# Softmax reciprocals applied to attention outputs by way of DRAM, with two steps of the feed-forward's side work moved

## The chip, the cores and the metric

The kernel runs on one core of a Trainium2 chip. The metric is the time of one execution in microseconds (us) on the device. Before the change three runs took 1823.91 to 1831.17 us, with a median of 1830.18.

The core has TensorE (PE; its weight loads are shown apart as PEld), VectorE (DVE), ScalarE (ACT), GpSimd (POOL) and SyncE (SP), which here only issues DMAs. The engines run side by side; each takes its own instructions in order and waits on semaphores.

## The reference

One encoder layer is applied with the same parameters to a prompt of 1024 tokens and a sample of 512, each token a row of 1024 float32. With a depth of 1 the layer is neighbourhood attention (16 heads of 64) followed by SwiGLU:

```
h = rms_norm(x, norm_mix)
x = x + neighbourhood_attention(h, w_qkv, rpb) @ w_o
x = x + swiglu(rms_norm(x, norm_ffn))        # (silu(a @ w_gate) * (a @ w_up)) @ w_down
y = rms_norm(x, norm_final)
```

Tokens lie on a grid 64 wide. A query sees a window of up to 8 rows by 16 columns of keys, with a bias per head and offset. For each head and query

```
s = q . k * scale + bias          (-inf outside the window)
p = softmax(s);   o = p @ v
```

## The kernel before, in words

**Precision.** Every matrix product is done in three passes on float32 operands split in two parts: a rounded high part (ACT casts) and the difference to the raw value (DVE subtracts, reading the raw and the high part). `split` (L139 to L145) does this, so most operands cost one ACT and one DVE instruction; L141 and L142 are those lines.

**V and the biases** come first (0 to 157 us): all V rows are computed and stored in DRAM (`v_d`), and the relative biases are laid out in DRAM as tables.

**Attention** (157 to 727 us) works on pairs of heads: eight pairs, each with two query groups of the prompt, then the eight pairs again with the one group of the sample. A group has two steps, so there are 32 prompt steps and 16 sample steps. A step handles two column blocks j of two heads each, that is four score tiles of 128 queries by 384 keys (256 in the sample). In `scores` (L391) the four tiles are computed on TensorE (`pss`, L397). For each tile DVE adds the bias, negates and takes the row minimum (L405), ACT takes the exponential with a row sum (L408), DVE takes the reciprocal of the row sum (L410), and the tile is multiplied by it, on DVE for the first head (L412) and on ACT for the second (L414). `flip` (L418) transposes the result on TensorE by 128x128 blocks (`ptt`, L423); ACT casts the high part out of PSUM (L426) and DVE takes the difference (L427). The score tiles and the transposed tiles come from the same pool of four PSUM banks (tag S), so the next step's scores wait until L427 has read the banks of this one.

In `step` (L477) the products with V of the *previous* step (`weighted`, L431, `po`) follow the scores of the present one, and `collect` (L438) puts the three parts of each head together: ACT copies one part into `tmp` (L444), DVE adds a second (L445) and the third (L447), the latter straight into `oT`, with 64 partitions for each head of the pair. Every second step POOL stores `oT` to `o_d` in DRAM (L462). `tmp` has two buffers.

Between these parts stand fillers on TensorE: the projections of the next pair's queries and keys (`pg`, L335), and in the sample stage the output projection of the prompt tokens (`pgo`, L593). They keep TensorE busy while the softmax is on its way.

`Chores` load raw weights and V rows ahead on SP's queue: four DMAs for a V job (L381), one for a weight block (L150). There are two raw buffers, so the next load starts when a split has freed one. Two bias tiles are loaded ahead on the same queue (L208 to L218), with a fill by POOL (L207, L211).

**The feed-forward** takes the tokens in two chunks of 768, each as two halves of 384, with the matrix products arranged after Winograd's form of Strassen's scheme: seven half-size products instead of eight, with sums and differences of operands (`operands`, L650) and of results. Each chunk has 11 units; a unit has 14 products (L822, 12 matmuls each), seven for the gate and seven for the up weights. Its results are multiplied (L885), summed on POOL (L889 to L892) and stored by seven DMAs that POOL issues (L894).

Side work runs between the products as generators. `ticks` (L911) gives such a generator one turn after every second product. In the first chunk's units these turns prepare the second chunk (`pair1`, L739): three pairs of token tiles; for each tile `norm2` (L672) loads the rows (L674, on ACT's queue), takes the squares (L677), the mean (L679, DVE), the root (L681, POOL) and the scaling (L683, ACT), and transposes (L690, L691); then the operands go to DRAM. In the last unit of the first chunk and around it they are reloaded as the second chunk's operands (`reload`, L899). In the second chunk's units the turns form the differences of the down weights (`down_sums`, L752): for each of 11 pairs of row blocks two loads, two DVE subtractions (L766, L768), two POOL subtractions (L771, L773) and two stores to `wt_d`, in five turns. From 1490 us on the down projection reads the stored products and weights back (L1066).

**What sets the order.** Each engine's instruction order is fixed when the program is built: the framework orders the traced instructions by its own estimate of when each can run, and the place in the program only decides between those that are ready. So work can run ahead of its place. In the first chunk, the loads of a pair's two tiles are five turns apart in the code, and the trace has them 1.43 us apart (950.34 and 951.77 us).

Of the kernel before, what the change touches and what calls it, by code (L numbers as in the profile page):

```python
# [18 lines left out]
P = 128  # L19
# [36 lines left out]
def body(tc, xp, xs, g_mix, g_ffn, g_fin, w_qkv, rpb, w_o, w_g, w_u, w_d, yp, ys):  # L56
# [9 lines left out]
    with es:  # L66
# [10 lines left out]
        o_d = dr.tile([HP, P, T], F32, name="o_d")  # L77
        x1_d = dr.tile([T, D], F32, name="x1_d")
# [312 lines left out]
        def scores(q, k, krow, nrow, j, bias):  # L391
            n = nrow * 32
            pss = [psum("S", "pss") for _ in range(2)]
            for i, (a, b) in enumerate(PASS):
                for h, pt in enumerate(pss):
                    kv = k[h * HD:(h + 1) * HD, b].rearrange("p (r c) -> p r c", c=GW)
                    nc.tensor.matmul(pt[:, :n], q[h * HD:(h + 1) * HD, a, j].rearrange("p r i -> p (r i)"),  # L397
                                     kv[:, krow:krow + nrow, BS[j]:BS[j] + 32],
                                     start=(i == 0), stop=(i == 2))
            yield  # L400
            out = []
            for h, pt in enumerate(pss):
                s = ap.tile([P, 384], F32, tag="s", name="s", bufs=4)
                mx = stat.tile([P, 1], F32, tag="mx", name="mx")
                nc.vector.tensor_tensor_reduce(s[:, :n], pt[:, :n], bias(h), -1.0, 3.0e38,  # L405
                                               ALU.add, ALU.min, accum_out=mx)
                sm = stat.tile([P, 1], F32, tag="sm", name="sm")
                nc.scalar.activation(s[:, :n], s[:, :n], AF.Exp, bias=mx, scale=-1.0, accum_out=sm)  # L408
                ri = stat.tile([P, 1], F32, tag="ri", name="ri")
                nc.vector.reciprocal(ri, sm)  # L410
                if h == 0:
                    nc.vector.tensor_scalar(s[:, :n], s[:, :n], ri, None, ALU.mult)  # L412
                else:
                    nc.scalar.mul(s[:, :n], s[:, :n], ri)  # L414
                out.append(s)
            yield out
# [21 lines left out]
        def collect(pos, dst):  # L438
            for h in range(2):
                m, o = (0, HD) if h == 0 else (HD, 0)  # L440
                pv = pos[h].rearrange("p (g z q) -> p g z q", g=2, z=2)
                tmp = ap.tile([P, 2, P], F32, tag="tmp", name="tmp")
# [3 lines left out]
                tv = t.rearrange("p g (r i) -> p g r i", i=16)  # L446
                nc.vector.tensor_tensor(dst(h), tv, pv[m:m + HD, :, 1].rearrange("p g (r i) -> p g r i", i=16),  # L447
                                        ALU.add)

        def steps(hp, g, q, k, v, n, store):  # L450
# [4 lines left out]
            for jj in range(2):  # L455
                sc = []
                for j in (jj * 2, jj * 2 + 1):
                    if j != 2:
                        b = next_bias()
                    sc.append(lambda b=b, j=j: scores(q, k, 4 * (g == 1), 4 * n, j, lambda h: b[:, h, :n * P]))  # L460
                yield dict(s=sc, n=n, jj=jj, v=v, dst=lambda h, jj=jj: ov[h * HD:(h + 1) * HD, jj * 2:jj * 2 + 2],
# [15 lines left out]
        def step(st, fill):  # L477

            sc = [x() for x in st["s"]] if st else []
            for x in sc:  # L480
                next(x)
            ss = [next(x) for x in sc]
            fill(0)
            if prev:
                p, pT = prev.pop()
# [3 lines left out]
                collect(pos, p["dst"])  # L489
# [6 lines left out]
            if st:  # L496
                prev.append((st, pT))
# [174 lines left out]
        def norm2(t, xn, xt):  # L672

            nc.scalar.dma_start(out=xn, in_=x1_d[t * P:(t + 1) * P, :])  # L674
            yield
            ms = stat.tile([P, 1], F32, tag="ms", name="ms")
            nc.scalar.activation(xt.rearrange("p k t -> p (k t)"), xn, AF.Square, accum_out=ms)  # L677
            me = stat.tile([P, 1], F32, tag="me", name="me")
            nc.vector.tensor_scalar(me, ms, 1.0 / D, EPS, ALU.mult, ALU.add)  # L679
            rs = stat.tile([P, 1], F32, tag="rs", name="rs")  # L680
            nc.gpsimd.tensor_tensor(rs, me, mhalf, ALU.pow)  # L681
            yield
            nc.scalar.mul(xn, xn, rs)  # L683
            yield
            for b in range(2):
                ks = slice(b * 4, b * 4 + 4)
                pt = psum("S", "pt")
                for kk in range(4):
                    k = b * 4 + kk
                    nc.tensor.transpose(pt[:, kk * P:(kk + 1) * P], xn[:, k * P:(k + 1) * P], ident)  # L690
                nc.vector.tensor_tensor(xt[:, ks], pt.rearrange("p (k t) -> p k t", k=4),  # L691
                                        gT[:, ks].rearrange("p (k o) -> p k o", o=1).to_broadcast([P, 4, P]),
                                        ALU.mult)
                yield

# [4 lines left out]
        def pair0(j):  # L700
            xs = []
            for t in (j, 3 + j):
                xn = np_.tile([P, D], F32, tag="xn", name="xn", bufs=3)
                xt = np_.tile([P, KB, P], F32, tag="xt", name="xt")
                for _ in norm2(t, xn, xt):
# [33 lines left out]
        def pair1(j):  # L739
            xs = []  # L740
            for n, t in enumerate((CT + j, CT + 3 + j)):
                xn = temp(2 * n)
                xt = temp(2 * n + 1).rearrange("p (k t) -> p k t", k=KB)
                yield from norm2(t, xn, xt)
                xs.append(xt)
# [188 lines left out]
        for p in range(NP):  # L934
            unit(1, p, hops2, tick if p else idle, None if 0 < p < NP - 1 else lambda n: None)
# [194 lines left out]
```

## Time and profile before

| | |
|---|---|
| median of three runs | 1830.18 us |
| the profiled execution | 1828.39 us |
| its span, first to last instruction | 1826.6 us |
| mean granted TensorE clock | 0.987 |
| attention, prompt | 157 to 484 us |
| attention, sample | 484 to 727 us |
| rest of the output projection, first chunk prepared | 727 to 797 us |
| gate and up products, both chunks | 797 to 1490 us |
| down projection and final norm | 1490 to 1819 us |

Times in rows of the profile are counted from the start of the span. A row of a group gives line, engine, operation, output and inputs with their shapes and the count, then the busy time in us and the mean of one in ns, then the engine's idle time just before these instructions and who ended it. A row of the timeline gives the start and the length in us; a bracket at its end gives the idle time before it and its releaser. A row of waits gives the total in us, how often, and the longest. The busy time of PE counts matmuls that overlap in the pipeline, so it does not show a slower pace. A releaser is inferred from semaphore events.

### The profile page before, as it was taken

Reading aid. Unit: us, or ns where it says so; the run is one execution under the profiler, and the core shown is the slowest. Engines: PE = TensorE matmul, PEld = TensorE weight load, DVE = VectorE, ACT = ScalarE, POOL = GpSimd, SP = SyncE. Lnnn points to the kernel's source line nnn. Section 1 sums busy time; section 2 is a strip of 40 time slices with the busy share of each in tenths; the row PEclk is TensorE's granted clock in tenths of the full one; section 3 lists DMA queues with packets and bytes.
Section 4 is the critical chain, followed back from the end, with each engine's and each line's share of the span. In section 5 each row is a group of like instructions: output and inputs, shape, how many; then the busy total and the mean of one; then the engine's idle time right before and its main releaser. Section 6 shows DMA issues by size and latency. Waiting matters only on the chain.

```text
span 1826.6 us, 25898 instructions
## 1 busy us (share of the span) xinstructions
PE 1755.7 (96%) x9178; PEld 1534.0 (84%) x9178; DVE 1222.2 (67%) x2263; ACT 869.9 (48%) x1742; POOL 441.4 (24%) x513
## 2 busy tenths in 40 slices
PE   7999999999999999999998999899999999999998
PEld 6887777777767878889998999899999988888886
DVE  4401887777887666667777877999777756546643
ACT  4411776767785554543443435433444435433423
POOL 1121000000130000103323343575424252005300
PEclk9999999999999999999999999899999999999999
DMA  7754333333465443643552635788343259645633
GB/s 242 220 187 157 108 108 101 104 117 108 125 203 155 139 145 121 196 162 120 173 167 93 209 107 168 257 295 287 112 136 122 78 191 322 194 153 165 215 103 107
DMA packets 229858, 295.60 MB, mean 162 GB/s; under 512 B 27648, under 2 KB 173824, under 8 KB 229728
## 3 DMA queue, kind: packets, MB, share of 16 engines
q1 hardware_dynamic: 205744, 215.94, 39.0%
q0 software_dynamic: 21248, 69.62, 10.4%
q10 hardware_dynamic: 2736, 8.39, 1.4%
q8 instruction: 72, 1.18, 0.3%
q14 instruction: 58, 0.48, 0.1%
HBM read 218.45 MB, written 87.97 MB: 168 GB/s over the span
## 4 chain that ended last, share of the span: by engine, by line
PE 69%; DVE 10%; DMA 9%; ACT 4%; issue 4%; POOL 2%; SPq 2%; DVEq 0%; ACTq 0%; POOLq 0%
PE pd L1066 17%; PE pa L822 15%; PE pg L335 8%; PE pd L822 7%; PE pgv L281 6%; PE pgo L593 5%; DMA vr<-v_d 4%; PE pb L822 4%; PE pss L397 3%; PE po L434 2%; PE ptt L423 2%; SPq L381 2%; DMA t<-ffn_w_down 1%; DMA wr<-na_w_qkv 1%; ACT s L408 1%
## 5 line engine op out<-in xcount | busy, mean ns | idle before, releaser
L1066 PE MATMUL pd<-wd,go 128*128 128x512 f32 x1386 | 324.7, 396 | 4.1 <-DVE wd L142 3.4
L1066 PEld LDWEIGHTS pd<-wd,go 128*128 128x128 f32 x1386 | 260.6, 188 | 68.0 <-DVE wd L142 4.8
L822 PE MATMUL pa<-h,ws 128*128 128x384 f32 x1056 | 202.9, 340 | 13.1 <-ACT c L847 10.7
L335 PE MATMUL pg<-hTp,whl 128*128 128x512 f32 x768 | 203.5, 409 | 0.0
L822 PEld LDWEIGHTS pa<-h,ws 128*128 128x128 f32 x1056 | 187.0, 191 | 16.4 <-ACT c L847 12.7
L822 PE MATMUL pd<-h,ws 128*128 128x384 f32 x1056 | 198.9, 336 | 0.1
L822 PEld LDWEIGHTS pd<-h,ws 128*128 128x128 f32 x1056 | 185.9, 189 | 0.5 <-ACT c L851 0.5
L142 DVE TENSOR_TENSOR ws<-wt,ws 128x1024 fp32r<-128x1024 f32 x88 | 114.7, 1304 | 96.7 <-ACT ws L141 96.5
L335 PEld LDWEIGHTS pg<-hTp,whl 128*128 128x128 f32 x768 | 140.4, 192 | 34.5 <-issue 7.7
L822 PE MATMUL pa<-h,wa 128*128 128x384 f32 x792 | 151.5, 344 | 9.3 <-DVE c L854 9.2
L822 PEld LDWEIGHTS pa<-h,wa 128*128 128x128 f32 x792 | 141.9, 192 | 12.3 <-DVE c L854 11.7
L593 PE MATMUL pgo<-wo,oh 128*128 128x512 f32 x576 | 138.9, 392 | 1.3 <-DVE oh L142 1.3
L141 ACT CAST go<-gr 128x768 fp32r<-128x768 f32 x84 | 65.6, 782 | 150.7 <-PE pd L1066 112.4
L408 ACT ACTIVATE s<-s,mx 128x384 f32<-128x384 f32 (+1 forms) x192 | 109.1, 570 | 54.3 <-DVE mx L405 54.1
L142 DVE TENSOR_TENSOR wa<-wr,wa 128x512 fp32r<-128x512 f32 x132 | 123.6, 948 | 11.5 <-ACT wa L141 10.4
L142 DVE TENSOR_TENSOR go<-gr,go 128x768 fp32r<-128x768 f32 x84 | 81.5, 971 | 71.6 <-ACT go L141 70.2
L894 POOL DMA_DIRECT2D gop_d<-c x66 | 50.6, 766 | 320.8 <-DVE c L885 315.9
L593 PEld LDWEIGHTS pgo<-wo,oh 128*128 128x128 f32 x576 | 107.4, 188 | 24.3 <-DVE oh L142 1.8
L141 ACT CAST wa<-wr 128x512 fp32r<-128x512 f32 x132 | 81.8, 621 | 92.4 <-PE pb L822 45.2
L141 ACT CAST ws<-wt 128x1024 fp32r<-128x1024 f32 x88 | 92.5, 1052 | 68.6 <-issue 47.0
L335 PE MATMUL pg<-hTs,whl 128*128 128x512 f32 x384 | 105.7, 411 | 1.6 <-DVE q L346 1.6
L822 PE MATMUL pb<-h,wa 128*128 128x384 f32 x528 | 101.3, 340 | 4.3 <-ACT wa L141 4.1
(159 smaller groups left out, 2954.4 us busy)
## 6 DMA issues: line engine op xcount, KB each, us to landing
wr<-ffn_w_gate SPq DMA_DIRECT2D x44, 512.0 KB
wr<-ffn_w_up SPq DMA_DIRECT2D x44, 512.0 KB
wr<-na_w_qkv SPq DMA_DIRECT2D x38, 512.0 KB
gop_d<-gs POOLq DMA_DIRECT2D x88, 192.0 KB, 5.8
gr<-gop_d SPq DMA_DIRECT2D x42, 384.0 KB
gr<-gop_d SPq DMA_DIRECT2D x42, 320.0 KB
gop_d<-c POOLq DMA_DIRECT2D x66, 192.0 KB, 2.5
vr<-v_d SPq DMA_DIRECT2D x192, 64.0 KB
```

The source lines that it names most:

```text
L141: nc.scalar.copy(hi, raw)
L142: nc.vector.tensor_tensor(lo, raw, f32(hi), ALU.subtract)
L281: nc.tensor.matmul(pg, hh[a][:, k, c:c + P], wv[k // 2][b][:, k % 2], start=(k == 0 and i == 0), stop=(k == KB - 1 and i == 2))
L335: nc.tensor.matmul(pg, w[:, a, k, :], h[b][:, k, c:c + 512], start=(k == 0 and i == 0), stop=(k == KB - 1 and i == 2))
L381: nc.sync.dma_start(out=raw[:, j * P:(j + 1) * P], in_=src[:, BS[j]:BS[j] + 32, :])
L397: nc.tensor.matmul(pt[:, :n], q[h * HD:(h + 1) * HD, a, j].rearrange("p r i -> p (r i)"), kv[:, krow:krow + nrow, BS[j]:BS[j] + 32], start ...
L408: nc.scalar.activation(s[:, :n], s[:, :n], AF.Exp, bias=mx, scale=-1.0, accum_out=sm)
L423: nc.tensor.transpose(pt[:, c * P:(c + 1) * P], s[:, c * P:(c + 1) * P], ident)
L593: nc.tensor.matmul(pg, ohs[k // 4][:, a, k % 4], wo[:, b, k, n * 512:(n + 1) * 512], start=(k == 0 and i == 0), stop=(k == KB - 1 and i == 2))
L822: nc.tensor.matmul(bank[:, :HT], a(y, k), b[:, z, k], start=start and k == 0 and i == 0, stop=k == KB // 2 - 1 and i == 2, skip_group_chec ...
L894: nc.gpsimd.dma_start(out=gop_d[i, 3 * c:3 * c + 3, :, p].rearrange("j q t -> q j t"), in_=a.rearrange("q (j t) -> q j t", j=3))
L1066: nc.tensor.matmul(pd, go[:, y, i - a], wds[m, i][:, z], start=(i == 0 and k == 0), stop=(i == NP - 1 and k == 2))
```

## The change

Three edits:

1. *Attention.* `scores` leaves the exponentials unnormalised and writes the four row sums of a step into one tile of 128x4. After the scores `reciprocals` takes all four reciprocals at once, stores them on SP's queue into a DRAM array `ri_d`, turned so that the queries lie along a row, and loads them back on the same queue into `rt`, one load for each head, with the row repeated on the head's 64 partitions. One step later `collect` adds the three parts in `tmp`, and POOL multiplies `tmp` by `rt` into `oT`. `tmp` has one buffer and holds both heads.
2. *Second chunk's preparation.* `norm2` takes a list of tiles. For a pair it loads both, then takes square, mean and root of each, leaves a turn empty, scales both, and then transposes both. A pair has 14 turns, as before.
3. *Down weights' differences.* The turns for `down_sums` begin with the third unit of the second chunk, not with the second.

```
 def scores(q, k, krow, nrow, j, bias, sm):
...
-                nc.scalar.activation(s[:, :n], s[:, :n], AF.Exp, bias=mx, scale=-1.0, accum_out=sm)
-                ri = stat.tile([P, 1], F32, tag="ri", name="ri")
-                nc.vector.reciprocal(ri, sm)
-                if h == 0:
-                    nc.vector.tensor_scalar(s[:, :n], s[:, :n], ri, None, ALU.mult)
-                else:
-                    nc.scalar.mul(s[:, :n], s[:, :n], ri)
+                nc.scalar.activation(s[:, :n], s[:, :n], AF.Exp, bias=mx, scale=-1.0, accum_out=sm[:, h:h + 1])
...
+        def reciprocals(sm, slot):
+            ri = stat.tile([P, 4], F32, tag="ri", name="ri")
+            nc.vector.reciprocal(ri, sm)
+            nc.sync.dma_start(out=ri_d[slot].rearrange("u h q -> q (u h)"), in_=ri)
+            rt = ap.tile([P, 2, P], F32, tag="rt", name="rt")
+            for h in range(2):
+                nc.sync.dma_start(out=rt[h * HD:(h + 1) * HD],
+                                  in_=ri_d[slot, :, h].rearrange("(o u) q -> o u q", o=1).to_broadcast([HD, 2, P]))
+            return rt
...
-        def collect(pos, dst):
+        def collect(pos, dst, rt):
+            tmp = ap.tile([P, 2, P], F32, tag="tmp", name="tmp", bufs=1)
             for h in range(2):
...
-                tmp = ap.tile([P, 2, P], F32, tag="tmp", name="tmp")
                 t = tmp[m:m + HD]
                 nc.scalar.copy(t, pv[o:o + HD, :, 0])
                 nc.vector.tensor_tensor(t, t, pv[m:m + HD, :, 0], ALU.add)
-                tv = t.rearrange("p g (r i) -> p g r i", i=16)
-                nc.vector.tensor_tensor(dst(h), tv, pv[m:m + HD, :, 1].rearrange("p g (r i) -> p g r i", i=16),
-                                        ALU.add)
+                nc.vector.tensor_tensor(t, t, pv[m:m + HD, :, 1], ALU.add)
+            nc.gpsimd.tensor_tensor(dst, tmp.rearrange("p g (r i) -> p g r i", i=16),
+                                    rt.rearrange("p g (r i) -> p g r i", i=16), ALU.mult)
...
-        def norm2(t, xn, xt):
+        def norm2(tiles):
+            rs = []
+            for t, xn, xt in tiles:
+                nc.scalar.dma_start(out=xn, in_=x1_d[t * P:(t + 1) * P, :])
+            yield
+            for t, xn, xt in tiles:
+                ms = stat.tile([P, 1], F32, tag="ms", name="ms")
+                nc.scalar.activation(xt.rearrange("p k t -> p (k t)"), xn, AF.Square, accum_out=ms)
+                me = stat.tile([P, 1], F32, tag="me", name="me")
+                nc.vector.tensor_scalar(me, ms, 1.0 / D, EPS, ALU.mult, ALU.add)
+                rs.append(stat.tile([P, 1], F32, tag="rs", name="rs"))
+                nc.gpsimd.tensor_tensor(rs[-1], me, mhalf, ALU.pow)
+                yield
+            yield
+            for (t, xn, xt), r in zip(tiles, rs):
+                nc.scalar.mul(xn, xn, r)
+                yield
+            for t, xn, xt in tiles:
+                for b in range(2):
...
         for p in range(NP):
-            unit(1, p, hops2, tick if p else idle, None if 0 < p < NP - 1 else lambda n: None)
+            unit(1, p, hops2, tick if p > 1 else idle, None if 0 < p < NP - 1 else lambda n: None)
```

54 lines of the change are left out of this document (21 added, 33 removed).

## Prediction

> **What bounds the kernel now.** I read the busy times of the page first, then the table by stages, then in each stage with idle time the waits of TensorE, and last the timeline around the longest of them.
>
> ```profile
> PE 1755.7 (96%) x9178; PEld 1534.0 (84%) x9178; DVE 1222.2 (67%) x2263; ACT 869.9 (48%) x1742; POOL 441.4 (24%) x513
> ```
> ```profile
> 157.00:484.00 327.00, 318.24 (x1799) 253.74 (x1797) 246.41 (x700) 219.74 (x534) 26.16 (x59) 0.99 0.38 114
> 484.00:727.00 243.00, 231.39 (x1257) 185.25 (x1257) 174.45 (x509) 147.58 (x386) 31.26 (x32) 0.99 0.48 147
> 860.00:1010.00 150.00, 141.53 (x794) 139.91 (x793) 109.84 (x150) 62.71 (x101) 54.00 (x58) 0.95 0.44 140
> 1110.00:1300.00 190.00, 175.90 (x968) 171.67 (x968) 171.11 (x192) 77.29 (x127) 109.18 (x91) 0.97 0.73 246
> 1300.00:1440.00 140.00, 140.00 (x805) 139.64 (x804) 102.64 (x134) 57.09 (x96) 51.13 (x54) 1.00 0.37 113
> ```
>
> TensorE is busy for 96% of the span, so only its stalls can be won. The second block is the table by stages (window, its length, then PE, PEld, DVE, ACT, POOL busy, granted clock, DMA share, GB/s): prompt attention, sample attention, the stage in which the second chunk is prepared, the change of chunks, and a quiet stretch for comparison. PE is idle for 8.8, 11.6, 8.5, 14.1 and 0.0 us in them. That is 43 us, and the three edits touch just these four stages. "Busy" hides more: after a stall the matmuls run slower for a while.
>
> ```profile
> 274.76 3.05 PE L335 MATMUL pg<-hTp,whl 128*128 128x512 f32 x12
> 284.57 2.19 PE L397 MATMUL pss<-kp,q 64*128 64x384 f32 x12 [0.84 <-DVE pT L427]
> 286.69 4.61 PE L335 MATMUL pg<-hTp,whl 128*128 128x512 f32 x12
> ```
>
> These rows lie two steps of prompt attention apart. Twelve projection matmuls take 3.05 us, and 4.61 us after a stall of 0.84 us, so that stall cost another 1.6 us; the granted clock of this stage is 0.99. The Trainium skill (TensorE: Matmul & The Clock Gate, "What's actually happening") says that the gate halves the clock after an idle window of about 3.4 us; here less idle time did it.
>
> **Attention: the waits and what feeds them.**
>
> ```profile
> PEld pss L397 <- DVE pT L427: 17.7, 40, 1.3
> PEld ptt L423 <- ACT s L414: 5.9, 11, 1.3
> ```
> ```profile
> PEld ptt L423 <- DVE s L412: 7.2, 7, 1.8
> PEld pss L397 <- DVE pT L427: 3.6, 9, 0.8
> PEld ptt L423 <- ACT s L414: 2.8, 6, 0.9
> ```
>
> The first pair is the prompt stage, the second block the sample stage: total wait, times, longest. The transposes (ptt) wait for the normalised scores of L412 and L414; the next scores (pss) wait for L427, which frees the PSUM tiles that they need. All five hang on one chain: scores, exp, reciprocal, multiplication, transpose, cast and difference. The edit takes two links out of it. At stake by these rows are 17.7 + 5.9 = 23.6 us in the prompt stage and 13.6 us in the sample stage. PEld waits partly under running matmuls, so the lower bound is PE's own idle time, 8.8 and 11.6 us, of which some belongs to other causes.
>
> **The change, attention.**
>
> ```profile
> L414 ACT ACTIVATE s<-s,ri 128x384 f32<-128x384 f32 (+1 forms) x96 | 52.8, 570 | 12.9 <-DVE ri L410 12.8
> L412 DVE TENSOR_SCALAR s<-s,ri 128x384 f32<-128x384 f32 (+1 forms) x96 | 39.7, 414 | 0.7
> L410 DVE RECIPROCAL ri<-sm 128x1 f32<-128x1 f32 x192 | 28.9, 157 | 18.5 <-ACT s L408 16.2
> L889 POOL TENSOR_TENSOR gs<-c 128x384 f32<-128x384 f32 x22 | 23.1, 1048 | 41.2 <-DVE c L885 41.2
> L891 POOL TENSOR_TENSOR gs<-c 128x384 f32<-128x384 f32 x22 | 31.9, 1451 | 0.0
> ```
>
> There are 48 steps (192 score tiles, four each). Removed: L414, 52.8 us of ACT, and L412, 39.7 us of DVE. The 192 reciprocals become 48, each of four columns: 48 × 157 ns = 7.5 us in place of 28.9. ACT gets 1.10 us a step lighter, DVE 61.1/48 = 1.27 us. Added on POOL: 48 products of 128x256. By two thirds of L889 and L891 one is 0.70 to 0.97 us; I take 0.85, the middle. POOL is busy for 26.16 of 327 us, so this is hidden.
>
> Will POOL slow DVE? It does where DVE reads two SBUF operands:
>
> ```profile
> L142 DVE TENSOR_TENSOR wa<-wr,wa 128x512 fp32r<-128x512 f32 x132 | 123.6, 948 | 11.5 <-ACT wa L141 10.4
> L142 DVE TENSOR_TENSOR oh<-wr,oh 128x512 fp32r<-128x512 f32 x24 | 16.3, 684 | 13.7 <-ACT oh L141 13.7
> L843 DVE TENSOR_TENSOR c<-c,pb 128x384 f32<-128x384 f32 x44 | 24.0, 546 | 6.9 <-PE pb L822 5.9 <-issue 1.0
> ```
> ```profile
> L142 DVE TENSOR_TENSOR v<-vr,v 128x512 fp32r<-128x512 f32 x30 | 20.5, 686 | 16.0 <-ACT v L141 15.9
> L145 DVE SCALAR_TENSOR_TENSOR whl<-wr,whl 128x1024 fp32r<-128x1024 f32 x8 | 9.7, 1208 | 0.3 <-ACT whl L144 0.3
> ```
>
> The same difference on 128x512 takes 684 ns beside a quiet POOL and 948 in the feed-forward stage, where POOL is busy for a third to over a half of the time (54.00 of 150 us, 109.18 of 190). In attention the operations with two SBUF operands are the splits of V and of the weights: 20.5 us for V and twice 9.7 for weights (L145, and as much for its sibling), 16% of DVE's 246.41. So of 48 × 0.85 = 41 us of POOL work some 7 us can fall on them; off the path mostly, I charge 1 us. The Trainium skill (SBUF — State Buffer, "Who interferes with whom") states it more harshly: where both read SBUF, the later of the two blocks fully. By it all 7 us would be lost and the sum below be 17 in place of 23; the row, 264 ns more on 684 with POOL busy for a third and more, agrees in kind.
>
> The two DMA directions go on SP. The reciprocals' write has 512 elements of 4 bytes; the two reads give each of 64 partitions the same rows.
>
> ```profile
> 274.63 2.23 SPq L381 DMA_DIRECT2D vr<-v_d  x4
> 276.97 0.60 SPq L212 DMA_DIRECT2D bp<-in_d  x1
> 280.59 0.62 ACT L141 CAST v<-vr 128x512 fp32r<-128x512 f32 x1 [1.91 <-DMA vr<-v_d]
> 282.16 0.87 DVE L445 TENSOR_TENSOR tmp<-tmp,po 64x256 f32<-64x256 f32 x2 [0.22 <-ACT tmp L444]
> 268.77 0.17 DVE L410 RECIPROCAL ri<-sm 128x1 f32<-128x1 f32 x1
> 0.74 0.43 SPq L95 DMA_DIRECT2D gT<-norm_ffn  x1
> ```
> ```profile
> o_d<-oT POOLq DMA_DIRECT2D x24, 256.0 KB, 2.3
> ```
>
> Issue: L95, a load of 1024 such elements, took 0.43 us, a bias load 0.60, so three are 1.6 us a step on a queue that holds some 4 us of work a step (a V job of 2.23 and about three bias loads). A store to DRAM lands in 2.3 us by the o_d row; a V load took 280.59 − 276.86 = 3.7 us after its last issue. The way there and back is then about 0.4 + 2.3 + 1.2 + 3.7 = 7.6 us. From the last reciprocal of a step (268.94) to its collection in the next (282.16) lie 13.2 us: hidden with 5 us to spare. If that cover is gone, the POOL product waits, and with it the o_d store and the bias memset queued on POOL; tmp, now single, is next written a whole step later.
>
> What isn't hidden: SP waits in order. The reads stand behind the write's landing, and V and weight loads queue behind the reads. ACT already waits 1.91 us for V in the step that ends in the 0.84 us stall. So the loads may come up to 2.3 + 1.2 = 3.5 us later in some steps, or not at all, where the build puts them ahead. Taken: 4 us of lost time in all, between −0 and +40.
>
> Gain: in the prompt stage half of 23.6, 12 us; in the sample stage, nearer to its PE idle share, 6 us of 13.6.
>
> **The change, second chunk's preparation.**
>
> ```profile
> 969.10 3.06 POOL L894 DMA_DIRECT2D gop_d<-gs  x4
> 972.17 0.56 POOL L681 TENSOR_TENSOR rs<-me,mhalf 128x1 f32<-128x1 f32 x1
> 972.77 1.15 ACT L683 ACTIVATE t<-t,rs 128x1024 f32<-128x1024 f32 x1 [2.81 <-POOL rs L681]
> 974.34 4.21 PE L822 MATMUL pa<-h,ws 128*128 128x384 f32 x12 [4.31 <-ACT c L847]
> 906.03 4.21 PE L822 MATMUL pa<-h,ws 128*128 128x384 f32 x12 [3.71 <-ACT c L847]
> 967.78 2.25 PE L822 MATMUL pd<-h,ws 128*128 128x384 f32 x12
> ```
>
> The root of tile two stands on POOL behind the unit's sums and DMA issues; ACT's scaling waits for it, the copy that frees the bank waits behind the scaling, and PE for the copy. It happens twice, 4.31 + 3.71 = 8.0 us, and each next product takes 4.21 us in place of 2.25: 11.9 us at stake. The edit loads both tiles, takes both squares and roots, leaves a turn, then scales. The second root so stands one turn behind the first, far ahead of the closing sums. The number of turns (14) and of operations is the same. I take two of three, 8 us; none is possible, and a new collision elsewhere as well, −3.
>
> **The change, down weights' differences later.** At 1110 to 1300 us DVE is busy for 171.11 of 190 us and PE idles 14.1; after 1300 DVE has room (102.64 of 140). The work moves one unit later in the program, but the build's own order ran it ahead before: the eleven rounds took 100 us, though their 55 turns, of two products of 2.25 us each, are 248 us.
>
> ```profile
> L766 DVE TENSOR_TENSOR t<-t x11: 677/679/694, 1162.0 to 1262.2; 128x512 f32<-128x512 f32 x11
> ```
>
> I take 2 us of the 14.1, with −4 to +7 as bounds.
>
> **Sum.** 12 + 6 + 8 + 2 − 4 − 1 = 23 us off. The profiled execution took 1828.4 us against a median of 1830.2, so 1805 for it and 1807 for the median. All gains at full and no cost: 23.6 + 13.6 + 11.9 + 7 = 56, 1774.
>
> **Rivals.** *SP's queue holds up V (slower).* For: ACT waits for V loads already, and DMAs that wait for one another go in between on the queue that brings V. Price: if half of the 48 steps pass on half of the 3.5 us, 24 × 1.75 = 42 us, less the other 28 gained: 1844. It decides from 28/48 = 0.6 us a step on PE's path. Against: V jobs are loaded two ahead, and no step of the chain needs the reciprocals soon.
> *The stall moves (no change).* The pT cast of the long step stands behind V's cast, and the V load sets that, with or without multiplications; a new order gives and takes some us elsewhere: 1829.
> *It doesn't do what it says.* The build reorders each engine's work, so the moved turns change nothing: only attention's 12 + 6 − 5 = 13 are left, 1817.
>
> **How the numbers follow.** Forecast 0.48, the third rival 0.14, no change 0.20, slower 0.18. A difference under 0.5% (9 us) can't be told from none here. The forecast, and the third rival nearly whole, are faster by more: 0.62; same 0.20; slower 0.18. The range runs from 1784, most of the gains, to 1838, which leaves out the worse half of the slow case and the largest gains; the forecast's own is 1784 to 1820.
>
> **What would show it.** Right: in the prompt stage the PEld waits for pT fall below half, ptt waits for exp alone, and twelve pg matmuls no longer take 4.6 us; DVE is some 55 us less busy; no ACT wait for L681's root over 1 us. Wrong: ACT's wait for V loads grows beyond its present 44.8 us, POOL waits for rt, or PE's idle time in the four stages stays at 43.
>
> ```profile
> ACT v L141 <- DMA vr<-v_d: 13.3, 10, 2.8
> ACT v L141 <- DMA vr<-v_d: 31.5, 11, 6.4
> ```

## The result, and the profile after

The changed kernel takes 2072.36 us (median of four runs, 2067.71 to 2074.91); the kernel before, beside it, 1827.39 us (1823.91 to 1831.17). The ratio is 1.134, with a 95% interval of 1.131 to 1.136. Not 23 us are gained: 245 are lost.

First the page of the kernel after: busy times, the packets, and the chain that ended last by engine and by line.

```profile
PE 1828.4 (88%) x9178; PEld 1582.7 (76%) x9178; DVE 1179.8 (57%) x2023; ACT 823.0 (40%) x1646; POOL 475.3 (23%) x561
DMA packets 269028, 302.01 MB, mean 146 GB/s; under 512 B 54528, under 2 KB 212992, under 8 KB 268896
...
PE 53%; DMA 23%; DVE 9%; issue 5%; SPq 4%; ACT 4%; POOL 1%; ACTq 0%; POOLq 0%; DVEq 0%
PE pd L1075 14%; PE pa L831 13%; DMA ri_d<-ri 8%; PE pd L831 6%; DMA vr<-v_d 6%; PE pg L336 6%; PE pgv L282 5%; PE pb L831 3%; SPq L382 2%; PE pgo L600 2%; PE pss L398 2%; DMA t<-ffn_w_down 1%; PE po L428 1%; SPq L439 1%; DMA wr<-na_w_qkv 1%
```

DVE and ACT did become lighter, by 42.4 and 46.9 us (the sign for it was some 55 for DVE). PE was busy for 96% of the span and is now for 88%. Its idle time rose from 70.9 to 244.7 us, and its busy time by 72.7 with the same 9178 matmuls: after stalls they run slower, as the prediction read in one place, and the mean granted clock fell from 0.987 to 0.930. The two together, 173.8 + 72.7, are the 246.5 us by which the span grew. The chain names the culprit in its third entry: the new store `ri_d<-ri` is 8% of the span, and loads of V, `vr<-v_d`, another 6%.

The table by stages of the kernel after (columns as before) says where:

```profile
157.00:668.00 511.00, 397.00 (x1985) 312.87 (x1983) 248.71 (x626) 214.57 (x536) 52.87 (x96) 0.83 0.37 90
668.00:985.00 317.00, 237.79 (x1110) 187.08 (x1108) 129.59 (x343) 106.40 (x286) 36.09 (x42) 0.85 0.48 105
1054.00:1736.00 682.00, 658.83 (x3747) 651.37 (x3745) 533.81 (x677) 289.63 (x474) 275.51 (x267) 0.99 0.52 169
```

The first sample scores now begin at 668.1 us and the last transposes of attention at 968.9, against 517.2 and 721.8 before, so the first two rows are the prompt's and the sample's attention. (The boundary of 484 us in the tables ahead so cuts the prompt's attention of the kernel before some 30 us short.) TensorE's idle time in the first is 114 us (511.00 − 397.00), and the granted clock in the two is 0.83 and 0.85, against 0.99 before. The first product of the feed-forward begins at 1054.4 us in place of 796.9, so 257 us were lost by then. The products of both chunks, the third row, take 682 us, less than the 693 of before (797 to 1490 us). All that was lost was lost in attention.

How one step loses it, in the timeline of the kernel after (SP, ACT and PE, one period of two steps):

```profile
303.12 0.53 SPq L436 DMA_DIRECT2D ri_d<-ri  x1
314.04 1.22 SPq L439 DMA_DIRECT2D rt<-ri_d  x2
315.37 2.26 SPq L382 DMA_DIRECT2D vr<-v_d  x4
321.82 0.62 ACT L142 CAST v<-vr 128x512 fp32r<-128x512 f32 x1 [9.90 <-DMA vr<-v_d]
323.25 1.63 ACT L420 CAST pT<-ptt 128x384 fp32r<-128x384 f32 x4
325.49 1.15 PE L398 MATMUL pss<-kp,q 64*128 64x384 f32 x3 [7.11 <-DVE pT L421]
```

SP issues the store at 303.12 and is done with that at 303.65. It then stands until 314.04, 10.4 us, before it may read the row back. Only then do the four loads of V go out. ACT, which has V's cast next in its fixed order, waits 9.90 us for them with the pT casts behind it; the pT tiles hold the banks that the next scores need; TensorE stands for 7.11 us. The chain is the one that the prediction named as a rival. Its size is another matter. SP's waits in attention (SPq stands for SP's queue), and three groups of the kernel after:

```profile
SPq L439 <- DMA ri_d<-ri: 369.5, 48, 11.0
```
```profile
L142 ACT CAST v<-vr 128x512 fp32r<-128x512 f32 x48 | 29.6, 619 | 233.1 <-DMA vr<-v_d 233.1
L452 POOL TENSOR_TENSOR oT<-tmp,rt 128x256 f32<-128x256 f32 x48 | 35.5, 740 | 444.3 <-DVE tmp L451 335.7
L435 DVE RECIPROCAL ri<-sm 128x4 f32<-128x4 f32 x48 | 8.5, 177 | 56.1 <-ACT s L408 55.8
```

SP waits in every one of the 48 steps, 7.7 us each by the first row. ACT's wait for V is 233.1 us, against 44.8 (13.3 + 31.5) before. From the end of the store's issue to the start of the next read's issue the median is 9.4 us (7.6 to 12.2); below this is called the store-to-read gap.

### The profile page after: what moved, and what is told of

Same layout as the page of the kernel before. It is cut to its first block, busy times and chain, and to the rows that moved or that the text cites. A ratio compares the mean times of both kernels' runs of the same rounds, so it can differ in the third digit from the quotient of the medians.

```text
span 2073.1 us, 26084 instructions
## 1 busy us (share of the span) xinstructions
PE 1828.4 (88%) x9178; PEld 1582.7 (76%) x9178; DVE 1179.8 (57%) x2023; ACT 823.0 (40%) x1646; POOL 475.3 (23%) x561
## 4 chain that ended last, share of the span: by engine, by line
PE 53%; DMA 23%; DVE 9%; issue 5%; SPq 4%; ACT 4%; POOL 1%; ACTq 0%; POOLq 0%; DVEq 0%
PE pd L1075 14%; PE pa L831 13%; DMA ri_d<-ri 8%; PE pd L831 6%; DMA vr<-v_d 6%; PE pg L336 6%; PE pgv L282 5%; PE pb L831 3%; SPq L382 2%; PE pgo L600 2%; PE pss L398 2%; DMA t<-ffn_w_down 1%; PE po L428 1%; SPq L439 1%; DMA wr<-na_w_qkv 1%
## 5 line engine op out<-in xcount | busy, mean ns | idle before, releaser
L336 PE MATMUL pg<-hTp,whl 128*128 128x512 f32 x768 | 223.9, 441 | 0.0
L336 PEld LDWEIGHTS pg<-hTp,whl 128*128 128x128 f32 x768 | 156.3, 213 | 42.9 <-issue 10.7
L398 PE MATMUL pss<-kp,q 64*128 64x384 f32 x384 | 75.5, 458 | 93.7 <-DVE pT L421 93.3
L600 PE MATMUL pgo<-wo,oh 128*128 128x512 f32 x576 | 143.7, 401 | 8.2 <-DVE xo L604 5.3
L398 PEld LDWEIGHTS pss<-kp,q 64*128 64x128 f32 x384 | 46.9, 233 | 120.6 <-DVE pT L421 111.8
L452 POOL TENSOR_TENSOR oT<-tmp,rt 128x256 f32<-128x256 f32 x48 | 35.5, 740 | 444.3 <-DVE tmp L451 335.7
L336 PE MATMUL pg<-hTs,whl 128*128 128x512 f32 x384 | 132.4, 490 | 3.7 <-ACT whl L145 3.5
L142 ACT CAST v<-vr 128x512 fp32r<-128x512 f32 x48 | 29.6, 619 | 233.1 <-DMA vr<-v_d 233.1
```

Of the source, the lines that this page charges most:

```text
L142: nc.scalar.copy(hi, raw)
L336: nc.tensor.matmul(pg, w[:, a, k, :], h[b][:, k, c:c + 512], start=(k == 0 and i == 0), stop=(k == KB - 1 and i == 2))
L452: nc.gpsimd.tensor_tensor(dst, tmp.rearrange("p g (r i) -> p g r i", i=16), rt.rearrange("p g (r i) -> p g r i", i=16), ALU.mult)
L600: nc.tensor.matmul(pg, ohs[k // 4][:, a, k % 4], wo[:, b, k, n * 512:(n + 1) * 512], start=(k == 0 and i == 0), stop=(k == KB - 1 and i == 2))
```

## The experiments

Four explanations were set against each other. **A:** SP's wait for the store to land holds up V's loads, as above, and that is all. **B:** POOL's product, with a single `tmp`, has become the bound. **C:** the two feed-forward edits cost. **D:** the store itself, waited for or not, slows the transfers behind it; **D1** says because its 4-byte pieces lie side by side in the same short stretch of DRAM, **D2** because of their number or size (512 pieces of 4 bytes). In the table below every ratio is to the kernel before, run beside it on the same chip, with its 95% interval.

| kernel | us | ratio | ACT's wait for V, us | gap, us |
|---|---|---|---|---|
| changed | 2072.4 | 1.134 (1.131–1.136) | 233.1 | 9.4 |
| changed, measured again later | 2030.7 | 1.114 (1.112–1.115) | 202.2 | 8.6 |
| attention edit alone | 2040.1 | 1.120 (1.116–1.123) | 205.9 | 8.6 |
| the same, again later | 2042.1 | 1.120 (1.118–1.122) | 201.2 | 8.4 |
| feed-forward edits alone | 1815.8 | 0.997 (0.995–0.998) | 42.8 | |
| reads that don't wait for the store | 1966.1 | 1.079 (1.076–1.082) | 151.2 | |
| before, with a store nobody reads | 1962.5 | 1.078 (1.076–1.080) | 117.2 | |
| pieces 8 bytes apart | 1863.0 | 1.021 (1.018–1.023) | 90.4 | 4.6 |
| pieces 64 bytes apart, read back | 1851.9 | 1.015 (1.013–1.018) | 75.3 | 2.9 |
| pieces 64 bytes apart, reads that don't wait for the store | 1818.0 | 0.999 (0.997–1.000) | 57.2 | |
| rows of 16 bytes, read back | 1825.6 | 1.002 (1.000–1.004) | 60.8 | 2.8 |
| rows of 16 bytes, reads that don't wait for the store | 1819.1 | 0.999 (0.997–1.000) | 52.7 | |
| turned on TensorE, rows of 512 bytes | 1824.8 | 1.002 (1.001–1.003) | 21.0 | 2.4 |
| the same, on POOL's queue | 1837.3 | 1.007 (1.005–1.010) | 41.1 | |
| the same, V's loads on two queues | 1830.8 | 1.004 (1.003–1.005) | 45.8 | |
| preparation alone | 1816.1 | 0.996 (0.995–0.998) | 44.2 | |
| preparation, V's loads on two queues | 1812.9 | 0.994 (0.993–0.996) | 44.7 | |

### Which edit costs

The changed kernel with the second and third edits undone:

```
-            yield from norm2([(CT + 3 * n + j, temp(2 * n), xs[n]) for n in range(2)])
+            for n, t in enumerate((CT + j, CT + 3 + j)):
...
+                yield from norm2(t, xn, xt)
...
-            unit(1, p, hops2, tick if p > 1 else idle, None if 0 < p < NP - 1 else lambda n: None)
+            unit(1, p, hops2, tick if p else idle, None if 0 < p < NP - 1 else lambda n: None)
```

> The attention edit alone; preparation and down weights as before the change. Theory A (the reciprocals' small store lands some 9 us after its issue, SP waits for it with the loads of V behind): nearly the whole loss, 2055 to 2085 us. Theory C (the two feed-forward edits, or the new order they bring, carry the loss): under 1900 us.

And the changed kernel with the first edit undone, that is, with attention as it was:

```
+                ri = stat.tile([P, 1], F32, tag="ri", name="ri")
+                nc.vector.reciprocal(ri, sm)
+                if h == 0:
+                    nc.vector.tensor_scalar(s[:, :n], s[:, :n], ri, None, ALU.mult)
+                else:
+                    nc.scalar.mul(s[:, :n], s[:, :n], ri)
...
-            rt = reciprocals(sm, st["slot"]) if st else None
```

> The two feed-forward edits alone; attention as before. Theory A: 1810 to 1835 us, and in the prediction's terms 10 us under the kernel before. Theory C: over 1950 us.

Measured: 2040.1 and 1815.8 us beside 1821.4 for the kernel before. Attention alone loses 219 us, some 15 less than the range expected for it, and the other two edits together gain 5.7 us. C falls.

That the attention edit alone lost less than the whole change (245) seemed to speak of a cost in combination. Both kernels were run again, unaltered, beside each other on one chip.

> The changed kernel as it is, beside the attention edit alone on the same chip. If the difference of 32 us between the two came from the chip (the reads followed the store after 9.4 us in one and 8.6 in the other): within 10 us of the attention edit alone, and 6 us under it rather than over. If the feed-forward edits make attention worse: 25 to 40 us over it.

> The attention edit alone again, the other half of the pair: 2030 to 2080 us by either reading; what tells is the difference, and the wait from store to read beside it.

Measured: 2030.7 and 2042.1 us. Beside each other the whole change is 11.4 us *faster* than its attention edit alone. What moved is the changed kernel itself: it took 2072 us with a gap of 9.37 us the first time and 2031 with 8.58 the second, and 48 × 0.79 = 38 us is nearly the difference of 42. The kernel before moved by 4 us between the two times. What makes the gap differ is open; it may be the chip.

### Wait or store

First the wait is taken away and the store kept. The two reads load from a weight vector of the input instead of from `ri_d`, so they need not wait for the store; the outputs are then scaled by numbers that aren't the reciprocals.

```
-                                  in_=ri_d[slot, :, h].rearrange("(o u) q -> o u q", o=1).to_broadcast([HD, 2, P]))
+                                  in_=g_mix[h * 256:(h + 1) * 256].rearrange("(o u q) -> o u q", o=1, u=2).to_broadcast([HD, 2, P]))
```

> The changed kernel with the same store, but the two reads take 256 values of an input array, so they wait for no store; the outputs are scaled by other numbers. Theory A: the loss is gone, 1790 to 1830 us. Theory B (POOL's product, the one tmp buffer or the later o_d store carry the loss): 2000 us or more. Theory D (the 512 pieces themselves hold the DMA engines): 1950 us or more.

Measured: 1966.1 us, 145 over the kernel before. SP no longer waits for the store at the reads, and still more than half of the loss is there. The reads aren't free of every wait, though: `rt` has two buffers, and a read must wait until POOL's product of two steps before has freed one.

```profile
SPq L439 <- POOL oT L452: 54.7, 35, 4.6
```

On the same chip the attention edit alone lost 219 us, and the feed-forward edits gained 6; of the 213 that should so be there some 68 went when the wait of 369.5 us for the store gave way to this shorter one. A, as the whole cause, seems to fall, but what is left needed a test without the rest of the edit: the kernel before, multiplications and all, with the four reciprocals of a step put in one tile and stored, and nobody reading them.

```
-                ri = stat.tile([P, 1], F32, tag="ri", name="ri")
+                ri = ri4[:, h:h + 1]
...
+            if st:
+                nc.sync.dma_start(out=ri_d[st["slot"]].rearrange("u h q -> q (u h)"), in_=ri4)
```

> The kernel before, with one thing added: the four reciprocals of a step lie in one tile, and that tile is stored on SP's queue as 512 pieces of 4 bytes, which nobody reads. Theory D (the store slows the transfers behind it on its queue, V's above all): 1920 to 1970 us, some 130 over the kernel before, as the run whose reads were free of the store. Theory A alone (only a wait for the store costs): 1820 to 1840 us.

Measured: 1962.5 us beside 1820.6. Forty-eight stores of 2 KB that nothing waits for cost 142 us, 3.0 us each. Theory D is shown with no part of the edit but the store and the tile that it is stored from, and A, as the whole cause, falls. Where it acts is seen in ACT's wait for V of that kernel, 44.8 us before:

```profile
L142 ACT CAST v<-vr 128x512 fp32r<-128x512 f32 x48 | 29.4, 622 | 117.5 <-DMA vr<-v_d 117.2
```

and, more surprisingly, in a store that goes by another queue. The row of DMA issues that gave the prediction its landing time, `o_d<-oT` on POOL's queue, says 2.3 us before. In the changed kernel, in this one, and in the one with rows of 16 bytes below it says:

```profile
o_d<-oT POOLq DMA_DIRECT2D x24, 256.0 KB, 9.0
```
```profile
o_d<-oT POOLq DMA_DIRECT2D x24, 256.0 KB, 8.3
```
```profile
o_d<-oT POOLq DMA_DIRECT2D x24, 256.0 KB, 2.8
```

The last column is the median from issue to landing. A store of 256 KB in long rows lands 6 us later because a store of 2 KB is on its way on SP's queue. So it isn't only SP's order that delays what follows; the small pieces hold up something that both queues share.

### What makes the store slow

The same 2 KB with each partition's four values side by side, 128 rows of 16 bytes instead of 512 of 4. Here a query gets another query's reciprocals.

```
-            nc.sync.dma_start(out=ri_d[slot].rearrange("u h q -> q (u h)"), in_=ri)
+            nc.sync.dma_start(out=ri_d[slot].rearrange("u h q -> (u h q)").rearrange("(q c) -> q c", c=4), in_=ri)
```

> The changed kernel with the reciprocals stored as 128 rows of 16 bytes in place of 512 elements of 4, and read back as before, so that the queries get one another's reciprocals. Theory A, landing set by the number or size of the pieces: the reads follow the write in 3 to 6 us in place of 9.4, and the time falls to 1850 to 1960 us. Landing set by something that every small store pays: 9 us still, 2050 us or more.

Measured: 1825.6 us, 4 over the kernel before and well under the range expected, where the changed kernel's attention edit had lost 219. SP's wait for the landing:

```profile
SPq L439 <- DMA ri_d<-ri: 66.9, 40, 3.7
```

That is 1.4 us a step in place of 7.7, for the same bytes, the same queue and the same dependence. But number, size and distance of the pieces all changed. In the next pair the reads don't wait for the store, as above. The first has 512 pieces of 4 bytes again, each in a 64-byte stretch of its own; the second has the rows of 16 bytes.

```
-        ri_d = dr.tile([HP * 6, 2, 2, P], F32, name="ri_d")
+        ri_d = dr.tile([HP * 6, P, 4, 16], F32, name="ri_d")
...
-            nc.sync.dma_start(out=ri_d[slot].rearrange("u h q -> q (u h)"), in_=ri)
+            nc.sync.dma_start(out=ri_d[slot, :, :, 0], in_=ri)
```

> As the run whose reads are free of the store, but the 512 pieces of 4 bytes go to places 64 bytes apart in DRAM, not side by side. Theory D1 (pieces that share a line of DRAM wait for one another): the loss is gone, 1800 to 1840 us. Theory D2 (the number or the size of the pieces): 1950 to 1980 us, no change.

> The changed kernel with both: the reciprocals stored as 128 rows of 16 bytes, and the reads from an input array, free of the store. What is left of the change is the lighter softmax, POOL's product, three DMAs a step and the feed-forward edits. If the prediction's gains in attention are there once the store is cheap and nothing waits: 1795 to 1812 us. If the gains were never there: 1818 to 1830 us.

Measured: 1818.0 and 1819.1 us, both 0.999 of the kernel before. The same number of 4-byte pieces that cost 145 us when packed cost nothing 64 bytes apart. B falls too as the cause of the loss, since both kernels have POOL's product and the single `tmp`. D2 falls and D1 stands: what is slow is several small pieces in one stretch of DRAM. One thing besides the distance was changed: the four pieces of a partition now follow one another in DRAM, where in the changed kernel the neighbours came from neighbouring partitions. The next two kernels keep the order of the changed kernel.

Two more kernels give the store a dependent read again, with 4-byte pieces 8 and 64 bytes apart. The reads take 128 adjacent values, so that they cost the same, and so mostly not the reciprocals; the array is filled once beforehand.

```
+        ri_d = dr.tile([HP * 6, 2, 2, P, 2], F32, name="ri_d")
...
+            nc.sync.dma_start(out=ri_d[slot, :, :, :, 0].rearrange("u h q -> q (u h)"), in_=ri)
...
+                                  in_=ri_d[slot, :, h, :64].rearrange("(o u) q x -> o u (q x)", o=1).to_broadcast([HD, 2, P]))
```

(16 in place of the last 2, and `:8` in place of `:64`, in the other.)

> The changed kernel with the 512 pieces stored 8 bytes apart, and reads that wait for the store but take 128 adjacent values of that space, so the outputs are scaled by other numbers. Theory D1 (pieces in one line of 64 bytes are written one after another): 8 in place of 16 to a line, so the reads follow the store after about half of 9.4 us, 4 to 6 us, and the time is 1840 to 1930 us. Theory E (pieces that touch each other are the trouble, not the count in a line): 2 to 3 us and 1820 to 1835 us.

> The same with 64 bytes between the pieces, one to a line. Theory D1: the reads follow the store after 1.5 to 2.8 us, no longer than with rows of 16 bytes, and the time is 1815 to 1830 us. If every small piece has a price of its own apart from its line: 5 us or more.

Measured: gaps of 4.65 and 2.89 us, beside 9.4 for the packed store and 2.8 for rows of 16 bytes. Sixteen pieces in 64 bytes, eight, and one: halving the neighbours about halves the gap. SP's waits of the two, in that order:

```profile
SPq L442 <- DMA ri_d<-ri: 141.2, 46, 5.3
```
```profile
SPq L442 <- DMA ri_d<-ri: 64.5, 37, 4.9
```

The times came to 1863.0 and 1851.9 us. The second is some 22 us above the range expected for it. Its SP wait is that of the rows of 16 bytes (64.5 against 66.9), but ACT waits 75.3 us for V, 14 more, and the `o_d` store lands in 3.6 us where it took 3.0 in the first kernel of the pair above; why is open, and the order of the pieces is one candidate. So that they cost nothing 64 bytes apart is shown only for the order of that kernel; that the gap shrinks with the distance is shown for the order of the change. Distances between 8 and 64 bytes weren't tried, so the length of the stretch isn't settled.

### The same computation with a quick store

If the packed 4-byte store is the fault, turning the reciprocals before they leave the chip mends it, with nothing left out of the computation. TensorE transposes the 128x4 tile, ACT copies it out of PSUM, and the store has four rows of 512 bytes.

```
+            pt = psum("S", "ptr")
+            nc.tensor.transpose(pt[:4, :P], ri, ident)
...
-            nc.sync.dma_start(out=ri_d[slot].rearrange("u h q -> q (u h)"), in_=ri)
+            nc.scalar.copy(rt[:4, 0], pt[:4, :P])
+            nc.sync.dma_start(out=ri_d[slot].rearrange("u h q -> (u h) q"), in_=rt[:4, 0])
```

> The changed kernel with the reciprocals turned by a TensorE transpose and an ACT copy (48 of each), then stored as four rows of 512 bytes; the reads wait for that store and give the right values. Theory A and D: landing as for large rows, so no loss: 1805 to 1835 us. If any store and load through DRAM holds SP: 1900 us or more.

Measured: 1824.8 us, 1.002 of the kernel before. The gap of 2.45 us is near the 2.3 us of the prediction. SP's wait for the landing:

```profile
SPq L442 <- DMA ri_d<-rt: 29.1, 32, 3.8
```

ACT's wait for V is 21.0 us, the shortest of all. So all but 4 of the 245 us come back, and still nothing is gained over the feed-forward edits alone (1.002 against 0.997). In attention TensorE's own waits (its own, not the weight loads') for pT and for the scores are, in the kernel before,

```profile
PE pss L397 <- DVE pT L427: 5.4, 7, 0.9
PE ptt L423 <- DVE s L412: 4.8, 5, 1.4
PE ptt L423 <- ACT s L414: 4.4, 13, 1.1
```

and in the kernel turned on TensorE, with the wait of the added transposition, which stands in TensorE's order and needs the reciprocal:

```profile
PE pss L398 <- DVE pT L421: 1.3, 1, 1.3
PE ptr L437 <- DVE ri L435: 22.0, 35, 2.3
```

The waits that the prediction wanted to win are down from 14.6 to 1.3 us, and a new one of 22.0 us stands in their place; how much of the old ones only moved into it wasn't tested. Two more tries to free the path: that kernel with the store and the reads on POOL's queue instead of SP's,

```
-            nc.sync.dma_start(out=ri_d[slot].rearrange("u h q -> (u h) q"), in_=rt[:4, 0])
+            nc.gpsimd.dma_start(out=ri_d[slot].rearrange("u h q -> (u h) q"), in_=rt[:4, 0])
...
-                nc.sync.dma_start(out=rt[h * HD:(h + 1) * HD],
+                nc.gpsimd.dma_start(out=rt[h * HD:(h + 1) * HD],
```

> The version with the reciprocals turned by a TensorE transpose and stored as rows of 512 bytes, with the store and both reads on POOL's queue in place of SP's; right values. If SP's order is what takes the attention gain away (V and weights wait behind the reads): 1800 to 1815 us. If the stall is set by V's own load, or by the DMAs' traffic: 1815 to 1830 us, as on SP's queue.

and with half of each V job's loads on POOL's queue:

```
-                nc.sync.dma_start(out=raw[:, j * P:(j + 1) * P], in_=src[:, BS[j]:BS[j] + 32, :])
+                (nc.sync if j < 2 else nc.gpsimd).dma_start(out=raw[:, j * P:(j + 1) * P], in_=src[:, BS[j]:BS[j] + 32, :])
```

> The version turned on TensorE (all three edits, right values), with V over two queues as well. If SP's crowded queue is what ate the softmax's gain: 1800 to 1815 us, under the 1825 of the same on one queue. If the gain isn't there: 1818 to 1830 us.

Measured: 1837.3 us, worse and over both ranges, and 1830.8 us, no better (1.004 against 1.002, with intervals that overlap). In the first, TensorE waits longer still for the added transposition:

```profile
PE ptr L437 <- DVE ri L435: 36.3, 40, 2.8
```

### The feed-forward edits apart

The kernel before with the reordered preparation alone, that is, with the second edit of the change as it stands, and the same with V's loads on two queues as above:

```
-                yield from norm2(t, xn, xt)
...
+            yield from norm2([(CT + 3 * n + j, temp(2 * n), xs[n]) for n in range(2)])
```

> The reordered preparation of the second chunk alone. By the prediction's terms 8 of the two edits' 10 us are its own: 6 us of the measured gain of both (ratio 0.9965) or more, ratio 0.995 to 0.998, and no ACT wait for the root over 1 us. If the later down weights carry the gain: 0.999 to 1.001.

> The reordered preparation, and two of the four DMAs of each V load issued by POOL in place of SP. If V's load sets the pace of attention: its issue ends 1.1 us sooner, ACT waits less than 42.8 us for V, and 3 to 10 us come off 1816. If it doesn't: 1812 to 1822 us.

Measured: 1816.1 us beside 1822.9, a ratio of 0.996 where both feed-forward edits gave 0.997: the down weights' later differences give nothing that can be seen, with intervals of 2.6 us to either side. In the stage of the second chunk's preparation, ACT's wait for the root and PE's for the copy are, before and with the reordered preparation,

```profile
ACT t L683 <- POOL rs L681: 5.6, 2, 2.8
```
```profile
PE pa L822 <- ACT c L847: 8.0, 2, 4.3
```
```profile
ACT t L688 <- POOL rs L684: 0.5, 2, 0.2
```
```profile
PE pa L824 <- ACT c L849: 4.0, 2, 2.5
```

The last kernel, at 1812.9 us and a ratio of 0.994, is the fastest version found and is faster than both the kernel before and the changed one. Its V wait didn't fall (44.7 us), so the 0.2% beyond the preparation, some 4 us between measurements on different chips, aren't explained by what was meant, and may be none.

## Why the prediction was wrong, step by step

**The step that failed first: "A store to DRAM lands in 2.3 us by the o_d row".** It measured 9.4 us from issue to read. The row was of 256 KB in long rows; the store was of 512 pieces of 4 bytes, and no row of the trace before showed such a store. The prediction did bound its issue by a load with as many elements, and that held (0.4 to 0.5 us); it didn't bound the landing, which it took from a row for another shape. The Trainium skill (DMA: Bandwidth & Descriptors, "Specifications") says that a transfer under 512 bytes makes the DMA engine read, modify and write. Taken alone that doesn't tell the cases apart: 4-byte pieces 64 bytes apart are as far below 512 bytes, and cost nothing where nobody waits for them (0.999). Whether the neighbours are slow because each rewrites the stretch that the last one wrote is a guess that fits the gaps of 9.4, 4.65 and 2.9 us, and wasn't shown.

**The step that wasn't there: the store's effect on others.** The sum had a term for waiting on the store and none for its presence. Alone, the store cost 142 us, where the whole change lost 207 (2030.7 against 1823.3) to 245. The landing of `o_d` on POOL's queue, up from 2.3 to 9.0 us, shows that the harm isn't bound to one queue, so that another queue for the store needn't have saved it; no run moved the packed store itself.

**"What isn't hidden", 4 us with bounds of 0 and 40, and the rival at 1844.** The mechanism, SP's order holding up V and V holding up the pT casts, was right, and the sign that the prediction named came: ACT's wait for V grew from 44.8 to 233.1 us. The size came from 3.5 us of delay, and half of it in half of the steps; SP's wait was 7.7 us on the mean, in all 48. What the mechanism costs with a quick store isn't measured by any pair of runs. With rows of 16 bytes, reads that wait for the store and reads that don't are 1.0022 against 0.9987, some 6 us; but SP stands about as long at the reads in both, 71 us and 82 us, in the second for POOL's product.

**"Hidden with 5 us to spare".** The way there and back, sized at 7.6 us, had 13.2 us of cover. With the gap of 9.4 it used up the cover in some steps: POOL waited 82.2 us in ten steps for `rt`, in all of attention.

```profile
POOL oT L452 <- DMA rt<-ri_d: 82.2, 10, 11.8
```

**"In the prompt stage half of 23.6, 12 us; in the sample stage 6".** Not seen in the time even where the store costs nothing. With rows of 16 bytes and reads that don't wait for the store the time is 0.999 of before, and the feed-forward edits without any attention edit have 0.997. The waits of TensorE's weight loads in the prompt stage of that kernel begin with:

```profile
PEld pss L398 <- DVE pT L421: 17.0, 44, 1.4
```

The transposes' waits for the scores, 5.9 us before, have nearly gone, as predicted. The larger wait, 17.7 us before, hasn't moved, and the timeline of that kernel shows why in one step:

```profile
278.68 0.62 ACT L142 CAST v<-vr 128x512 fp32r<-128x512 f32 x1 [2.37 <-DMA vr<-v_d]
279.33 0.76 ACT L449 COPY tmp<-po 64x256 f32<-64x256 f32 x2
280.11 1.63 ACT L420 CAST pT<-ptt 128x384 fp32r<-128x384 f32 x4
282.36 1.84 PE L398 MATMUL pss<-kp,q 64*128 64x384 f32 x9 [0.97 <-DVE pT L421]
```

This is the long step of before again, 0.97 us of stall in place of 0.84. V's load, not the multiplications, was what came last in it. That was the rival "The stall moves", which the prediction had at 0.20 and for which it had quoted the row (1.91 us of waiting for V in that step); the 12 us were taken from the sums of waits all the same. What made that load late isn't settled. Its DMAs stood on SP's queue behind reads of `rt`, which went out right after POOL's product had ended (269.82 + 0.74 us); the last row has all such waits of SP in that kernel:

```profile
269.82 0.74 POOL L452 TENSOR_TENSOR oT<-tmp,rt 128x256 f32<-128x256 f32 x1 [4.70 <-DMA ri_d<-ri]
270.59 1.14 SPq L439 DMA_DIRECT2D rt<-norm_mix  x2
271.83 3.48 SPq L382 DMA_DIRECT2D vr<-v_d  x4
```
```profile
SPq L439 <- POOL oT L452: 81.9, 43, 5.5
```

The prediction had no term for reads that wait for POOL's product, and no run gave `rt` a third buffer. Where V is in time, in the kernel turned on TensorE (21.0 us), TensorE's waits for pT and for the scores do nearly go, and the added transposition takes their place. The sample's first scores do begin earlier, at 509.7 us against 515 to 517 with the old attention, but the first feed-forward product begins at 797.8 against 790 to 797: the sample stage gives it back. Why it is longer there is open; its granted clock was 0.96 in place of 0.99, and ACT waits 35.6 us for V and 17.5 for `whl` weights there, against 31.5 and 7.7 before, all of it loaded on SP's queue.

**"I take two of three, 8 us"** for the preparation was right: 6.9 us measured, with the waits for root and copy down by the 5.1 and 4.0 us above. **"I take 2 us of the 14.1"** for the down weights: none seen, but 2 us is within the intervals. **POOL's product** at 0.85 us measured 0.740, within its bounds; TensorE doesn't wait for it, but SP's reads do, as said. The four reciprocals at once took 177 ns (157 taken).

## What to carry to other kernels

Size a DMA by a row with the same pieces on the same side: a store of 2 KB in neighbouring 4-byte pieces lands four times later than 256 KB in long rows, and delays what other queues send. If a small tile must leave the chip turned, turn it first (or spread the pieces out), and charge a store for its presence as well as for who waits on it. Before counting a wait as won by a shorter chain, look in the timeline at what else ends just before it: with rows of 16 bytes a load of V stood in the same place, and the shorter chain left the wait at 17.0 us.

## What the runs showed of the hardware

- Packed 4-byte pieces: 9.4 us from store to read; 8 bytes apart 4.65; 64 bytes apart 2.9; rows of 16 bytes 2.8; rows of 512 bytes 2.45 (SP's queue, medians).
- Their harm crosses queues: the landing of a store on POOL's queue went from 2.3 to 8.3 us beside stores on SP's queue that nobody read. The Trainium skill (DMA: Bandwidth & Descriptors, "Anatomy of one DMA — SWDGE (gpsimd) path") puts the fixed cost of a DMA that GpSimd issues at some 2 us, most of it the receipt of the write. The gaps here are on SP's queue: those of 2.45 to 2.9 us are near that, those of 4.65 and 9.4 aren't.
- The cost of such a store differs between measurements far more than the rest of the kernel: 2072 and 2031 us for the same changed kernel, 1827 and 1823 for the one before.
